# Sampled tokens' high and low parts in one stationary operand: two matmuls instead of three

## The chip, the cores and the metric

The kernel runs on one core of one Trainium2 chip. The metric is the device time of one execution in microseconds. Before the change it was 3355.91 us (median of 3 runs, 3352.63 to 3362.21).

## The reference

One step of a one-layer decoder. There are 2048 prompt tokens and 64 sampled tokens (8 sequences of 8), with a model width of 1024. Both kinds of tokens go through the same weights:

```python
z  = x @ w_in                                  # q, k, v, gates of two kinds of heads
fox_h = softmax(q k^T * scale + decay) @ v     # sampled tokens: over 8192 cached positions, paged
m_h   = mLSTM(q, k, v, gates)                  # chunked matrix memory
x1  = layer_norm(ALPHA * x  + concat(fox_h, norm(m_h) * og) @ w_o)
hid = square(relu(x1 @ w1))                    # width 4096
y   = layer_norm(ALPHA * x1 + hid @ w2)
```

Outputs are `y` for prompt and sampled tokens, the new keys, values and gates, and the memory's states.

## The kernel before

**Precision by three matmuls.** Every operand of a large product is split into a high part in a shorter float format (`split_hi`, an ACT copy, L149) and a low part, the difference (`split_lo`, a DVE subtraction, L152). A product is then made of three matmuls into the same PSUM buffer (`mm3`, L157 to L159): high by high, high by low, low by high. Each matmul has a weight load of its own (PEld in the profile) for the stationary operand, which has one column for each row of the result.

**Tiles.** Prompt tokens make 16 tiles of 128 rows (t = 0 to 15). The 64 sampled tokens are tile 16. Where tokens are the stationary operand, tile 16 uses 64 of the 128 columns.

**Stages.** Block A (`block_a`, four blocks of prompt tokens; the first, `BLKS[0]`, starts with tile 16) makes the input products. Eight passes through `natural` have tokens as the stationary operand and 256 or 272 weight columns moving: two for the memory's values, two for the output gate, two for keys, two for values. For each tile the results go through a PSUM buffer `pm` (four in rotation) to `sink`, which evicts them with ACT (`stage`) or DVE. Between these passes lie eight convolution passes and four query passes with weights as the stationary operand. Phase B is the prompt's attention, phase O its output projection. Phase C is the MLP in four blocks of tiles (`CB`; only the last, 12 to 15, contains tile 16). For each of 16 chunks `fc` of the hidden width, `hidden` (L1382 on) makes 2 x 128 hidden columns, transposed, with the split parts in `hh` and `hl`; `output` (L1398 on) multiplies the chunk before by `w2` for every tile in two halves of 512 columns into a buffer `py` (three in rotation) and adds it to the tile's row `y` (L1422). The last two chunks are put out together, tile by tile, with the layer norm behind each tile; tile 16, the last, has a layer norm of its own in two halves (`last_norm`), whose halves leave from SP's and ACT's queues.

**The sampled tokens' output projection** (`sampled`, L1343 on) stands in the third block of phase C, ahead of its chunk 14, when the sampled attention is done. It uses 8 pieces of `w_o` through the raw buffers `wr` (four) and the split buffers `wh` and `wl`, 4 x 8 products of 256 columns, and a layer norm.

**The sampled attention** (`sample_attention`) is a stream of steps that is put between the matmuls of all other stages at a given pace. Its cached keys come by indirect DMA from POOL's queue (L1597) into a ring `kT`, are transposed by DVE (L1603) and multiplied on PE (L1626); values come the same way (L1714, L1738). A small tile `ri` for the decay uses the ring's memory first.

**Order.** A scheduler orders the instructions of each engine when the kernel is built; buffers that rotate decide who waits for whom.

Of the kernel before, what the change touches and what calls it, by code (L numbers as in the profile page):

```python
# [10 lines left out]
F32 = mybir.dt.float32  # L11
# [3 lines left out]
OP = mybir.AluOpType  # L15
# [37 lines left out]
def body(ctx, tc, I, O, stages):  # L53
# [102 lines left out]
    def mm3(ps, wh, wl, xh, xl, first, stop):  # L156
        T.matmul(ps, wh, xh, start=first, stop=False)  # L157
        T.matmul(ps, wh, xl, start=False, stop=False)  # L158
        last["PE"] = T.matmul(ps, wl, xh, start=False, stop=stop)  # L159

    def layer_norm(x, np_, g, b, wk, tg, eng=None):
        w = wk.tile([128, 64], F32, name="ln", bufs=2)
        st, mv, rs = w[:, 0:12].rearrange("p (i s) -> p i s", i=2), w[:, 16:18], w[:, 24:27]
        for i in range(2):
            V.bn_stats(st[:np_, i], x[:, i * 512:(i + 1) * 512])
        V.bn_aggr(mv[:np_], st[:np_])
        V.tensor_scalar(rs[:np_, 0:1], mv[:np_, 1:2], EPS, None, op0=OP.add)
# [3 lines left out]
        V.tensor_tensor(x, x, g[:np_], op=OP.mult)  # L171
        (eng or G).tensor_tensor(x, x, b[:np_], op=OP.add)
# [33 lines left out]
    pz = es_z.enter_context(tc.tile_pool(name="pz", bufs=1, reuse_waits="tile"))  # L206
    es_a = ExitStack()
    pa = es_a.enter_context(tc.tile_pool(name="pa", bufs=1, reuse_waits="tile"))
    ppa = es_a.enter_context(tc.tile_pool(name="ppa", bufs=1, space=PSUM, reuse_waits="tile"))


# [253 lines left out]
    def block_a(bi):  # L465
# [3 lines left out]
        def natural(sink, *cols, hook=None, after=None):  # L469
            wh, wl = W0.pop() if W0 else wload(cols)  # L470
            for i, t in enumerate(blk):
                if hook:
                    hook(i)
                m = tok_n(t)
                ps = ppa.tile([128, 512], F32, name="pm", tag="pm", bufs=4)[:m, :wh[0].shape[1]]
                (xh, xl), s = xcol(bi, t)
                for k in range(8):
                    mm3(ps, xh[:, k, s], xl[:, k, s], wh[k], wl[k], k == 0, k == 7)
# [5 lines left out]
        def stage(ps, m, n):  # L484
            st = pa.tile([128, 256], F32, name="st", bufs=4)[:m, :n]
            A.copy(st, ps)
            return st

        def turn_next(n):
# [5 lines left out]
        for i in range(2):  # L495
            def sink(t, m, ps, i=i):
                r = tok_r(t)
                SY.dma_start(dv[r:r + m, i * 256:(i + 1) * 256], stage(ps[:, :256], m, 256))
                if i == 1:
                    V.tensor_copy((gats if t == 16 else gat[:, t])[:, 0:16], ps[:, 256:272])  # L500
# [76 lines left out]
        for i in range(2):  # L577
            def sink(t, m, ps, i=i):
                r = tok_r(t)
                cs = slice(i * 256, (i + 1) * 256)  # L580
                st = pa.tile([128, 256], F32, name="st", bufs=4)[:m]
                V.tensor_tensor(st, ps, bog[:m, cs], op=OP.add)
# [28 lines left out]
        for i in range(2):  # L611
            def sink(t, m, ps, i=i):
                d = k_out(t)[:, i * 256:(i + 1) * 256]
                if t == 16:
                    if i == 0:
                        sqk.append(ps_.tile([64, 512], F32, name="sqk", tag="vt", bufs=2))
                    st = sqk[0][:, i * 256:(i + 1) * 256]
                    A.copy(st, ps)
# [302 lines left out]

    gen = None
    if "S" in stages:
        gen = sample_attention(tc, I, O, ps_, pps, cst, ident, sqk, dnl, dR, dmix, dqb, vx, kx, pa)
    x_load(16, 0)
    W0 = [wload([(C_V, 256)])]
    x_turn(0, 16)
# [404 lines left out]
    def phase_c():  # L1332
# [10 lines left out]
        def sampled():  # L1343

            mx = pc.tile([128, 8, 64], F32, name="mxs", tag="hq", bufs=1)
            SY.dma_start(mx, dmv[:, :, S:])
            mh = ph.tile([128, 8, 64], F32R, name="mhs", tag="hh", bufs=4)
            ml = ph.tile([128, 8, 64], F32R, name="mls", tag="hl", bufs=4)
            split_hi(mh, mx)
            split_lo(ml, mx, mh)  # L1350
            y = row()
            SY.dma_start(y[:64], x_of(16))
            for c in range(4):
                ps = ppc.tile([128, 512], F32, name="py", bufs=3)[:64, :256]
# [5 lines left out]
                V.scalar_tensor_tensor(y[:64, s], y[:64, s], ALPHA, ps, op0=OP.mult, op1=OP.add)  # L1360
            layer_norm(y[:64], 64, *vecs(1), pc, "1")
            SY.dma_start(dx1[S:], y[:64])

# [7 lines left out]
        for ci, blk in enumerate(CB):  # L1371
# [7 lines left out]
            def hidden(fc):  # L1379
                w1p = C.pop("w1", None) or w1_pieces(fc)  # L1380
                H[fc] = []
                for f in range(2):  # L1382
                    hh = ph.tile([128, 576], F32R, name="hh", bufs=4)
                    hl = ph.tile([128, 576], F32R, name="hl", bufs=4)
                    H[fc].append((hh, hl))
                    for (a, b) in pieces:
                        ps = ppc.tile([128, 512], F32, name="ph", tag="ph", bufs=3)[:, :b - a]
                        for k in range(8):
# [3 lines left out]
                        A.activation(hq, ps, AF.Relu)  # L1392
                        A.activation(hq, hq, AF.Square)
                        split_hi(hh[:, a:b], hq)
                        split_lo(hl[:, a:b], hq, hh[:, a:b])
                        tick((b - a) * 0.01)

            def output(fcs):  # L1398
                w2p = [piece(w2[fc * 256 + k * 128:fc * 256 + k * 128 + 128].rearrange("(k p) c -> p k c", p=128)) for fc in fcs for k in range(2)]
                h = [x for fc in fcs for x in H.pop(fc)]  # L1400
                if 15 in fcs:
                    gb = vecs(2)
                for t in blk:
                    n = tok_n(t)
                    s = slice(off[t], off[t] + n)
                    if 0 in fcs:
                        ys[t] = row()
                        with tc.issue_after(last["ACT"].ins):
                            A.dma_start(ys[t][:n], dx1[tok_r(t):tok_r(t) + n])
                    for hf in range(2):  # L1410
                        cs = slice(hf * 512, (hf + 1) * 512)
                        ps = ppc.tile([128, 512], F32, name="py", bufs=3)[:n]
                        for k in range(len(h)):
                            wh, wl = (x[:, 0, cs] for x in w2p[k])
                            mm3(ps, h[k][0][:, s], h[k][1][:, s], wh, wl, k == 0, k == len(h) - 1)
                        y = ys[t][:n, cs]
                        if 15 in fcs and t == 16 and hf == 1:
                            last_norm(ys[t][:n], n, *gb, pc, ps, O["y_sample"].rearrange("b t d -> (b t) d"))
# [5 lines left out]
                    if 15 in fcs and t < 16:  # L1424
                        layer_norm(ys[t], n, *gb, pc, "2")
                        SY.dma_start(O["y_prompt"][0, t * 128:(t + 1) * 128], ys[t])

            for fc in range(16):
                if fc == 14:
# [27 lines left out]
    es_s.close()  # L1457


def sample_attention(tc, I, O, ps_, pps, cst, ident, sqk, dnl, dR, dmix, dqb, vx, kx, pa):  # L1460

    nc = tc.nc
    V, A, G, T, SY = nc.vector, nc.scalar, nc.gpsimd, nc.tensor, nc.sync
# [393 lines left out]
```

## Time and profile before

| what | value |
|---|---|
| time, median of 3 runs | 3355.91 us |
| lowest, highest | 3352.63, 3362.21 us |
| profiled execution: span (the page has no other time of it) | 3381.2 us |
| PE busy, matmuls | 3266.7 us, 21564 |
| PE weight loads busy | 2623.4 us |
| DVE busy | 2145.9 us |
| ACT busy | 1413.8 us |
| POOL busy | 869.5 us |
| mean granted clock of PE | 0.988 |

The span is that of one execution with the profiler on. Matmuls overlap, so a matmul's listed duration is longer than the distance to the next one. "L157" is line 157 of the kernel before. In rows of a timeline the columns are start, duration, engine, line, operation, result<-inputs, shapes and count; in brackets stands how long the engine had nothing to do before, and what released it. In grouped rows the numbers are the total busy time, the mean in ns, and the idle time before with its releasers. A row "128*64 128x512" of a matmul has a stationary operand of 64 columns and 512 moving columns.

### The profile page before, as it was taken

What the parts mean: (1) busy time and instruction counts of PE and PEld (TensorE: products, weight loads), DVE (VectorE), ACT (ScalarE), POOL (GpSimd) and SP (SyncE); (2) the same over time, 40 slices, a digit from 0 to 9 for tenths busy, and PEclk for the clock granted to TensorE, in tenths of its full rate; (3) what the DMA queues carried; (4) which work ended last, traced back from release to release, by engine and by line L of the source; (5) the groups of instructions that cost most, each with busy time, mean ns of one, the idle gap of its engine ahead of it and who ended that gap; (6) DMA issues with size and microseconds to landing.
All of it is one profiled execution on the core that took longest, in us unless ns stands there. A gap on an engine that the chain in (4) does not pass through costs nothing. (4 is left out here: it accounts for less than half of the span.)

```text
span 3381.2 us, 57759 instructions
## 1 busy us (share of the span) xinstructions
PE 3266.7 (97%) x21564; PEld 2623.4 (78%) x21564; DVE 2145.9 (63%) x5180; ACT 1413.8 (42%) x2989; POOL 869.5 (26%) x928
## 2 busy tenths in 40 slices
PE   9999999999999999999999999999999999999998
PEld 8998897787866667677777776777777777888886
DVE  5857567556478878655666667666676545644545
ACT  4444245334378888422332333232332323433332
POOL 0112122422332222365423324323243110100001
PEclk9999999999999999999999999999999999999999
DMA  5665765866652322587776768767678545532221
GB/s 172 165 189 179 221 206 180 292 212 219 227 166 81 90 76 61 209 283 245 286 249 244 247 226 299 254 234 270 209 258 289 198 164 160 168 103 83 87 76 66
DMA packets 427232, 646.25 MB, mean 191 GB/s; under 512 B 83148, under 2 KB 320016, under 8 KB 426056
## 3 DMA queue, kind: packets, MB, share of 16 engines
q1 hardware_dynamic: 350184, 363.22, 35.3%
q0 software_dynamic: 74304, 270.57, 21.8%
q10 hardware_dynamic: 2464, 8.78, 0.7%
q8 instruction: 170, 2.79, 0.3%
q14 instruction: 110, 0.90, 0.1%
HBM read 589.63 MB, written 52.83 MB: 190 GB/s over the span
## 5 line engine op out<-in xcount | busy, mean ns | idle before, releaser
L1422 DVE TENSOR_TENSOR y<-y,py 128x512 f32<-128x512 f32 (+1 forms) x475 | 320.5, 681 | 310.7 <-PE py L159 287.4
L149 ACT ACTIVATE wh<-wr 128x1024 fp32r<-128x1024 f32 x268 | 278.1, 1056 | 500.8 <-PE py L159 215.3
L159 PE MATMUL ph<-x1h,wl 128*128 128x512 f32 (+1 forms) x1280 | 452.9, 355 | 7.7 <-DVE wl L152 7.1
L157 PE MATMUL ph<-x1h,wh 128*128 128x512 f32 (+1 forms) x1280 | 454.9, 355 | 3.6 <-ACT wh L149 2.9
L1597 POOL DMA_INDIRECT kT<-cache_k,idxK x256 | 272.5, 1064 | 718.2 <-PE sQ L1626 657.7
L158 PE MATMUL ph<-x1l,wh 128*128 128x512 f32 (+1 forms) x1280 | 454.4, 355 | 0.0
L1603 DVE STREAM_TRANSPOSE kT<-kT 128x512 f32<-128x512 f32 x512 | 330.3, 685 | 177.1 <-DMA kT<-cache_k,idxK 170.5
L157 PE MATMUL py<-wh,hh 128*128 128x512 f32 (+1 forms) x1088 | 431.7, 399 | 6.8 <-DVE y L1420 4.0
L158 PE MATMUL py<-wl,hh 128*128 128x512 f32 (+1 forms) x1088 | 426.4, 392 | 0.6 <-issue 0.6
L159 PE MATMUL py<-wh,hl 128*128 128x512 f32 (+1 forms) x1088 | 426.3, 393 | 0.3 <-issue 0.3
L152 DVE TENSOR_TENSOR wl<-wr,wh 128x1024 fp32r<-128x1024 f32 x268 | 335.0, 1256 | 81.5 <-ACT wh L149 28.6
L157 PE MATMUL pm<-whi,xhT 128*128 128x256 f32 (+2 forms) x1088 | 319.0, 293 | 4.6 <-ACT whi L149 1.7
L158 PE MATMUL pm<-wlo,xhT 128*128 128x256 f32 (+2 forms) x1088 | 313.8, 289 | 0.8 <-DVE wlo L152 0.8
L159 PE MATMUL pm<-whi,xlT 128*128 128x256 f32 (+3 forms) x1088 | 313.5, 288 | 0.0
L157 PEld LDWEIGHTS ph<-x1h,wh 128*128 128x128 f32 x1280 | 241.8, 189 | 42.9 <-issue 5.2
L159 PEld LDWEIGHTS ph<-x1h,wl 128*128 128x128 f32 x1280 | 241.8, 189 | 43.0 <-DVE wl L152 9.4
L158 PEld LDWEIGHTS ph<-x1l,wh 128*128 128x128 f32 x1280 | 241.9, 189 | 36.9 <-issue 4.1
L157 PEld LDWEIGHTS py<-wh,hh 128*128 128x128 f32 (+1 forms) x1088 | 201.3, 185 | 64.4 <-issue 11.9
L159 PEld LDWEIGHTS py<-wh,hl 128*128 128x128 f32 (+1 forms) x1088 | 200.9, 185 | 52.7 <-issue 5.3
L158 PEld LDWEIGHTS py<-wl,hh 128*128 128x128 f32 (+1 forms) x1088 | 201.4, 185 | 40.6 <-issue 2.3
L157 PEld LDWEIGHTS pm<-whi,xhT 128*128 128x128 f32 (+1 forms) x1088 | 207.9, 191 | 13.7 <-issue 7.8
L1072 ACT ACTIVATE S<-S,mx 128x512 f32<-128x512 f32 (+2 forms) x320 | 207.8, 652 | 17.7 <-DVE mx L1060 16.6
(394 smaller groups left out, 6534.9 us busy)
## 6 DMA issues: line engine op xcount, KB each, us to landing
wr<-w SPq DMA_DIRECT2D x256, 512.0 KB
wra<-w_in SPq DMA_DIRECT2D x112, 512.0 KB
Rb<-dR SPq DMA_DIRECT2D x128, 128.0 KB
wr<-w_o SPq DMA_DIRECT2D x16, 512.0 KB
xr<-dmix SPq DMA_DIRECT2D x16, 512.0 KB
y<-x_prompt SPq DMA_DIRECT2D x16, 512.0 KB
dx<-y SPq DMA_DIRECT2D x16, 512.0 KB
xr<-dx SPq DMA_DIRECT2D x16, 512.0 KB
```

The lines of the kernel that those rows point to most:

```text
L149: last["ACT"] = A.activation(dst, src, AF.Copy, scale=scale)
L152: r = (eng or V).tensor_tensor(dst, src, hi.bitcast(F32), op=OP.subtract)
L157: T.matmul(ps, wh, xh, start=first, stop=False)
L158: T.matmul(ps, wh, xl, start=False, stop=False)
L159: last["PE"] = T.matmul(ps, wl, xh, start=False, stop=stop)
L1072: last["ACT"] = A.activation(sp[:, :w], sp[:, :w], AF.Exp, bias=mx[:, 7:8], accum_out=lp[:, k:k + 1])
L1422: V.tensor_tensor(y, y, ps, op=OP.add)
L1597: G.indirect_dma_start(out=piece(n), out_offset=None, in_=ck, in_offset=IO(ap=idxK[:, b, j // 2, j % 2:j % 2 + 1], axis=0))
L1603: V.transpose(x, x)
```

## The change

For tile 16 the high and the low part stand side by side as 64 + 64 columns of one stationary operand. Two matmuls, with the weights' high part and with their low part, then give the products of the high part in PSUM rows 0 to 63 and those of the low part (low by low with them) in rows 64 to 127. The two halves are added behind.

```diff
+    def mm2(ps, whl, xh, xl, first, stop):
+        T.matmul(ps, whl, xh, start=first, stop=False)
+        last["PE"] = T.matmul(ps, whl, xl, start=False, stop=stop)
...
+    pe = es_e.enter_context(tc.tile_pool(name="pe", bufs=1, reuse_waits="tile"))
+    def ring_a():
+        es_e.close()
+        pr = es_a.enter_context(tc.tile_pool(name="pr", bufs=1, reuse_waits="tile"))
+        return pr.tile([128, 2, 2, 1024], F32, name="kT", bufs=1)
...
+            xT["s"] = pe.tile([128, 8, 128], F32R, name="xsT")
...
+            if t == 16:
+                for c, x in enumerate((xh, xl)):
+                    G.tensor_copy(xT["s"][:, hf * 4:hf * 4 + 4, c * 64:c * 64 + 64], x[:, hf * 4:hf * 4 + 4, s])
...
+                    if t == 16 and xT["s"] is not None:
+                        mm2(ps, xT["s"][:, k], wh[k], wl[k], k == 0, k == 7)
+                    else:
+                        mm3(ps, xh[:, k, s], xl[:, k, s], wh[k], wl[k], k == 0, k == 7)
...
-            A.copy(st, ps)
+            A.copy(st, ps[:m])
+            if m < ps.shape[0]:
+                V.tensor_tensor(st, st, ps[64:128], op=OP.add)
...
         kx["new"] = True
+        xT["s"] = None
...
-        ri = pa.tile([128, 8, 129], F32, name="ri", tag="kT", bufs=1)
+        ri = pe.tile([128, 8, 129], F32, name="ri", bufs=1)
...
-    kx["ring"] = pa.tile([128, 2, 2, 1024], F32, name="kT", tag="kT", bufs=1)
+    kx["ring"] = ring_a()
...
-                        mm3(ps, mh[:, kg * 4 + k], ml[:, kg * 4 + k], wh[:, k], wl[:, k], kg + k == 0, kg + k == 4)
+                        mm2(ps, mhl[:, kg * 4 + k], wh[:, k], wl[:, k], kg + k == 0, kg + k == 4)
...
+                V.tensor_tensor(y[:64, s], y[:64, s], ps[64:128], op=OP.add)
...
-                    hh = ph.tile([128, 576], F32R, name="hh", bufs=4)
-                    hl = ph.tile([128, 576], F32R, name="hl", bufs=4)
-                    H[fc].append((hh, hl))
+                    h2 = ph.tile([128, 1152], F32R, name="h", bufs=4)
+                    hh, hl = h2[:, 0:576], h2[:, 640:1152]
+                    H[fc].append((hh, hl, h2[:, 512:640]))
...
-                        split_lo(hl[:, a:b], hq, hh[:, a:b])
+                        e = min(b, 512)
+                        split_lo(hl[:, a:e], hq[:, :e - a], hh[:, a:e])
+                        if b > 512:
+                            split_lo(h2[:, 576:640], hq[:, e - a:], hh[:, e:b])
...
-                for t in blk:
+                for t in (blk[-1:] + blk[:-1] if 15 in fcs and ci == 3 else blk):
...
+                        if t == 16:
+                            V.memset(ys[t][64:128], 0.0)
...
+                            if t == 16:
+                                mm2(ps, h[k][2], wh, wl, k == 0, k == len(h) - 1)
+                            else:
+                                mm3(ps, h[k][0][:, s], h[k][1][:, s], wh, wl, k == 0, k == len(h) - 1)
...
-                        if 15 in fcs and t == 16 and hf == 1:
+                        if 15 in fcs and t == 15 and hf == 1:
...
+                    if 15 in fcs and t == 16:
+                        lo = landing(64)
+                        A.copy(lo, ys[t][64:128])
+                        V.tensor_tensor(ys[t][:64], ys[t][:64], lo, op=OP.add)
```

In the MLP the low rows are summed in rows 64 to 127 of tile 16's `y` over all chunks, and added once at the end (by way of ACT, to the other partitions). In the last output group tile 16 comes first and tile 15 last, and `last_norm` serves tile 15. The two value passes keep three matmuls, since the joint operand's memory is given to the ring of keys (`ring_a`) after the key passes. The gates' and the output gate's evictions get an addition of the same kind as `stage`.

More of the change, by code (lines that the diff above doesn't have):

```diff
@@ L474, in natural @@
                 m = tok_n(t)
-                ps = ppa.tile([128, 512], F32, name="pm", tag="pm", bufs=4)[:m, :wh[0].shape[1]]
+                ps = ppa.tile([128, 512], F32, name="pm", tag="pm", bufs=4)[:m if xT["s"] is None else 128, :wh[0].shape[1]]
                 (xh, xl), s = xcol(bi, t)
                 for k in range(8):
-                    mm3(ps, xh[:, k, s], xl[:, k, s], wh[k], wl[k], k == 0, k == 7)
+                    if t == 16 and xT["s"] is not None:
+                        mm2(ps, xT["s"][:, k], wh[k], wl[k], k == 0, k == 7)
+                    else:
+                        mm3(ps, xh[:, k, s], xl[:, k, s], wh[k], wl[k], k == 0, k == 7)
                 sink(t, m, ps)
@@ L482, in natural, with stage @@
                 tick(2.6)
-        def stage(ps, m, n):
-            st = pa.tile([128, 256], F32, name="st", bufs=4)[:m, :n]
-            A.copy(st, ps)
+        def stage(ps, m, n, st=None):
+            if st is None:
+                st = pa.tile([128, 256], F32, name="st", bufs=4)[:m, :n]
+            A.copy(st, ps[:m])
+            if m < ps.shape[0]:
+                V.tensor_tensor(st, st, ps[64:128], op=OP.add)
             return st
@@ L499, in sink @@
                 if i == 1:
-                    V.tensor_copy((gats if t == 16 else gat[:, t])[:, 0:16], ps[:, 256:272])
+                    V.tensor_copy((gats if t == 16 else gat[:, t])[:, 0:16], ps[:m, 256:272])
+                    if t == 16:
+                        V.tensor_tensor(gats, gats, ps[64:128, 256:272], op=OP.add)
             natural(sink, (C_V + i * 256, 256), *([(C_FF, 8), (C_I, 8)] if i == 1 else []),
@@ L581, in sink @@
                 st = pa.tile([128, 256], F32, name="st", bufs=4)[:m]
-                V.tensor_tensor(st, ps, bog[:m, cs], op=OP.add)
+                V.tensor_tensor(st, ps[:m], bog[:m, cs], op=OP.add)
+                if m == 64:
+                    V.tensor_tensor(st, st, ps[64:128], op=OP.add)
                 A.activation(st, st, AF.Tanh, scale=0.5)
@@ L616, in sink @@
                         sqk.append(ps_.tile([64, 512], F32, name="sqk", tag="vt", bufs=2))
-                    st = sqk[0][:, i * 256:(i + 1) * 256]
-                    A.copy(st, ps)
+                    st = stage(ps, m, 256, sqk[0][:, i * 256:(i + 1) * 256])
                 else:
@@ L923, in body @@
     if "S" in stages:
-        gen = sample_attention(tc, I, O, ps_, pps, cst, ident, sqk, dnl, dR, dmix, dqb, vx, kx, pa)
+        gen = sample_attention(tc, I, O, ps_, pps, cst, ident, sqk, dnl, dR, dmix, dqb, vx, kx, pe, ring_a)
     x_load(16, 0)
@@ L1346, in sampled @@
             SY.dma_start(mx, dmv[:, :, S:])
[L1347 to L1350, printed above, removed]
+            mhl = ph.tile([128, 8, 128], F32R, name="mhs", tag="h", bufs=4)
+            split_hi(mhl[:, :, 0:64], mx)
+            split_lo(mhl[:, :, 64:128], mx, mhl[:, :, 0:64])
             y = row()
@@ L1353, in sampled @@
             for c in range(4):
-                ps = ppc.tile([128, 512], F32, name="py", bufs=3)[:64, :256]
+                ps = ppc.tile([128, 512], F32, name="py", bufs=3)[:, :256]
                 for kg in range(2):
@@ L1409, in output @@
                             A.dma_start(ys[t][:n], dx1[tok_r(t):tok_r(t) + n])
+                        if t == 16:
+                            V.memset(ys[t][64:128], 0.0)
                     for hf in range(2):
                         cs = slice(hf * 512, (hf + 1) * 512)
-                        ps = ppc.tile([128, 512], F32, name="py", bufs=3)[:n]
+                        ps = ppc.tile([128, 512], F32, name="py", bufs=3)
                         for k in range(len(h)):
                             wh, wl = (x[:, 0, cs] for x in w2p[k])
-                            mm3(ps, h[k][0][:, s], h[k][1][:, s], wh, wl, k == 0, k == len(h) - 1)
-                        y = ys[t][:n, cs]
-                        if 15 in fcs and t == 16 and hf == 1:
-                            last_norm(ys[t][:n], n, *gb, pc, ps, O["y_sample"].rearrange("b t d -> (b t) d"))
+                            if t == 16:
+                                mm2(ps, h[k][2], wh, wl, k == 0, k == len(h) - 1)
+                            else:
+                                mm3(ps, h[k][0][:, s], h[k][1][:, s], wh, wl, k == 0, k == len(h) - 1)
+                        y = ys[t][:, cs]
+                        if 15 in fcs and t == 15 and hf == 1:
+                            last_norm(ys[t], n, *gb, pc, ps, O["y_prompt"][0, t * 128:(t + 1) * 128])
                         elif 0 in fcs:
@@ L1423, in output @@
                         tick(1.28 * len(fcs))
-                    if 15 in fcs and t < 16:
-                        layer_norm(ys[t], n, *gb, pc, "2")
-                        SY.dma_start(O["y_prompt"][0, t * 128:(t + 1) * 128], ys[t])
+                    if 15 in fcs and t == 16:
+                        lo = landing(64)
+                        A.copy(lo, ys[t][64:128])
+                        V.tensor_tensor(ys[t][:64], ys[t][:64], lo, op=OP.add)
+                    if 15 in fcs and (t, ci) != (15, 3):
+                        layer_norm(ys[t][:n], n, *gb, pc, "2")
+                        SY.dma_start(O["y_sample"].rearrange("b t d -> (b t) d") if t == 16 else O["y_prompt"][0, t * 128:(t + 1) * 128], ys[t][:n])
             for fc in range(16):
@@ L1457, in body, with sample_attention @@
     es_s.close()
-def sample_attention(tc, I, O, ps_, pps, cst, ident, sqk, dnl, dR, dmix, dqb, vx, kx, pa):
+def sample_attention(tc, I, O, ps_, pps, cst, ident, sqk, dnl, dR, dmix, dqb, vx, kx, pe, ring_a):
     nc = tc.nc
```

3 lines of the change are left out of this document (2 added, 1 removed).

## The prediction

> **What bounds the kernel now.** I read the page's busy shares first, then a table of stages, then the order of time inside the stages that the change touches.
>
> ```profile
> span 3381.2 us, 57759 instructions
> PE 3266.7 (97%) x21564; PEld 2623.4 (78%) x21564; DVE 2145.9 (63%) x5180; ACT 1413.8 (42%) x2989; POOL 869.5 (26%) x928
> core 0: us, PE busy (x) PEld busy (x) DVE busy (x) ACT busy (x) POOL busy (x), PEclk, DMA share, GB/s
> 60.00:80.00 20.00, 20.00 (x151) 19.39 (x150) 18.84 (x50) 11.27 (x31) 0.00 (x0) 1.00 0.35 84
> 3000.00:3366.00 366.00, 366.00 (x2127) 321.77 (x2126) 188.20 (x265) 121.30 (x210) 9.32 (x7) 1.00 0.25 76
> ```
>
> PE is busy for 97% of the span. The page warns that a busy PE is not PE at its peak, so the stage table matters more. From 3000 to 3366 us, which is the MLP of the last block (the only one with the sampled tile), PE is busy 366.00 of 366.00 us at clock 1.00. DVE has 188.20 us of work there and the DMA share is 0.25. Whatever leaves PE in that stage leaves the time, as long as the matmuls that remain keep their pitch. Early in the kernel it is otherwise: between 60 and 80 us DVE is busy 18.84 of 20 us, so DVE is nearly as tight as PE there.
>
> The timed median is 3355.91 us. The profiled execution shows no time of its own but its span of 3381.2 us, 25.3 us (0.75%) above that median. I make the sum against the span and scale the result by 3355.91/3381.2 = 0.9925.
>
> **MLP output, 64 matmuls fewer.** A matmul's own duration overlaps its neighbours', so its cost is the pitch, the distance of starts. The first pair of rows is three steps apart with a stationary operand of 64 columns, the second three steps apart with 128 columns. Both have 512 moving columns.
>
> ```profile
> 3329.70 0.39 PE L159 MATMUL py<-wh,hl 128*64 128x512 f32 x1
> 3330.38 0.39 PE L159 MATMUL py<-wh,hl 128*64 128x512 f32 x1
> 3342.63 0.39 PE L159 MATMUL py<-wh,hl 128*128 128x512 f32 x1
> 3343.31 0.39 PE L159 MATMUL py<-wh,hl 128*128 128x512 f32 x1
> L158 PEld LDWEIGHTS py<-wl,hh 128*128 128x128 f32 x1024 | 192.8, 188 | 37.3 <-issue 2.3
> L158 PEld LDWEIGHTS py<-wl,hh 128*64 128x64 f32 x64 | 8.6, 134 | 3.3
> ```
>
> Both pitches are 0.68/3 = 0.227 us: the moving columns set it, and the wider load (188 ns against 134 ns) stays beside the matmul before it. The sampled tile has 16 chunks x 2 pieces x 2 halves = 64 products; each loses one of three matmuls. Gain: 64 x 0.227 = 14.5 us, all in the stage where PE never pauses.
>
> **Six input passes.** These rows are 22 steps apart in both pairs, with 256 moving columns: first 64 stationary columns, then 128.
>
> ```profile
> 104.81 0.28 PE L158 MATMUL pm<-wlo,xhT 128*64 128x256 f32 x1
> 107.31 0.28 PE L159 MATMUL pm<-whi,xlT 128*64 128x256 f32 x1
> 15.02 0.28 PE L158 MATMUL pm<-wlo,xhT 128*128 128x256 f32 x1
> 17.66 0.28 PE L159 MATMUL pm<-whi,xlT 128*128 128x256 f32 x1
> ```
>
> That is 0.1136 and 0.120 us. A pass of the sampled tile goes from 24 x 0.1136 = 2.73 us to 16 x 0.120 = 1.92 us: 0.81 us gained. [...]
>
> Not all six gains last. In the first pass the pitch is another (eight steps between the first two rows), and the second pass and the stage behind it wait for something that PE does not set:
>
> ```profile
> 10.34 0.41 PE L157 MATMUL pm<-whi,xhT 128*64 128x256 f32 x1
> 12.05 0.41 PE L159 MATMUL pm<-whi,xlT 128*64 128x256 f32 x1
> 29.55 1.11 ACT L149 ACTIVATE whi<-wra 128x1088 fp32r<-128x1088 f32 x1 [3.72 <-DMA wra<-w_in]
> 30.71 0.46 PE L157 MATMUL pm<-whi,xhT 128*64 128x272 f32 x2 [0.94 <-ACT whi L149]
> 92.27 0.19 PE L456 MATMUL mg<-ident,rows 4*64 4x4 f32 x1 [2.51 <-DVE rows L422]
> L981 POOL COPY dup<-dup 128x256 f32<-128x256 f32 x31 | 12.5, 405 | 62.0 <-DMA dup<-k_prompt 46.9 <-PE po L1094 12.4 <-PE pS L1046 2.6
> ```
>
> The first pass could give 8 x 0.214 = 1.7 us. But the second pass's weights come at 29.55 by DMA and PE already waits 0.94 us for them, so that wait would grow by as much. What the second pass gains (0.8 us) runs into the stage where DVE is full and PE waits 2.51 us for it. I take 0 for these two passes; the other bound is -2.5 us. The four POOL copies that fill the joint operand (405 ns each, by the row of that size, 1.6 us together) lie ahead of the first pass, under the same wait for weights. The four later passes (two gate, two key passes, from 104 us on) I count in full: 4 x 0.81 = 3.2 us. Their extra DVE adds follow the tile that comes first in each pass, with four PSUM buffers in rotation, so nobody waits for them.
>
> **Output projection.** 96 matmuls become 64: 96 x 0.1136 - 64 x 0.120 = 3.2 us, if PE bounded it.
>
> ```profile
> 2863.08 2.70 SPq L1196 DMA_DIRECT2D wr<-w_o  x2
> 2868.88 1.06 ACT L149 ACTIVATE wh<-wr 128x1024 fp32r<-128x1024 f32 x1 [1.21 <-DMA wr<-w_o]
> 2869.14 18.78 SPq L1196 DMA_DIRECT2D wr<-w  x7
> 2874.08 0.28 PE L159 MATMUL py<-wh,mls 128*64 128x256 f32 x1
> 2876.26 0.50 PE L157 MATMUL ph<-x1h,wh 128*128 128x512 f32 x1 [1.91 <-ACT wh L149]
> 2878.00:2880.00 2.00, 2.00 (x6) 1.52 (x6) 1.88 (x4) 0.00 (x0) 0.00 (x0) 0.50 0.66 182
> L1360 DVE SCALAR_TENSOR_TENSOR y<-y,py 64x256 f32<-64x256 f32 x4 | 1.6, 406 | 0.0
> ```
>
> The last w_o piece is split at 2868.88, when its DMA lands, and the next w1 load leaves SP at 2869.14, when that stage's splits free a raw buffer; neither waits for these matmuls. PE's last product starts at 2874.08 and PE then stands 1.91 us until w1 is there. Three microseconds saved ahead of this only lengthen that stand. I take 0, between -3.2 us (buffers that come free sooner bring w1 forward by as much) and +1.6 us (the four added DVE evictions, 406 ns each by the row of the present ones, stand ahead of splits). After this stand the clock falls to 0.50 between 2878 and 2880. [...]
>
> **More DVE work in the last block.** Each second low part is split into 224 and 64 columns.
>
> ```profile
> L152 DVE TENSOR_TENSOR hl<-hq,hh 128x288 fp32r<-128x288 f32 x64 | 29.2, 457 | 65.0 <-ACT hh L149 63.1
> L361 DVE TENSOR_TENSOR gt<-gt,gat 128x64 f32<-128x64 f32 x4 | 0.9, 222 | 0.0
> ```
>
> 224 columns cost between 457 x 224/288 = 355 and 457 ns, the 64 columns 222 ns: at most 32 x 0.22 = 7 us more on DVE over the block, which had 178 us free in 366. It is hidden by matmuls. Without that cover 7 us would come back.
>
> **The end.** The sampled tile moves to the front of the last output group, and tile 15 with 128 rows is the last.
>
> ```profile
> 3366.05 0.40 PE L159 MATMUL py<-wh,hl 128*64 128x512 f32 x1
> 3371.39 0.99 POOL L183 TENSOR_TENSOR ln<-ln,nhalf 64x1 f32<-64x1 f32 x1
> 3372.56 1.40 DVE L188 SCALAR_TENSOR_TENSOR y<-y,ln,b 64x512 f32<-64x512 f32 x2
> 3373.99 0.52 ACTq L189 DMA_DIRECT2D y_sample<-y  x1
> L172 POOL TENSOR_TENSOR y<-y,b 128x1024 f32<-128x1024 f32 x32 | 78.7, 2458 | 54.5 <-DVE y L171 52.5 <-DVE ln L167 1.9
> 2892.00:2896.00 4.00, 4.00 (x19) 3.30 (x19) 3.25 (x5) 3.15 (x6) 0.00 (x0) 1.00 0.95 341
> ```
>
> Now the last matmul starts at 3366.05, the power on POOL at 3371.39, the last issue is at 3373.99 and the span ends 7.2 us later. In the built lists of the changed kernel two POOL additions of 2.46 us stand directly ahead of that power, and tile 13's scaling on DVE waits for tile 14's statistics; following the chain by hand with these durations puts the final scaling 6.9 us behind the last matmul instead of 6.5: I say +0.6 us. Twice the bytes, 256 KB more at the fastest rate of these rows, 341 GB/s, are 0.75 us, of which I leave 0.25 to the time between the two issues: +0.5. At the front of that group the sampled tile's two PSUM buffers and tile 12's are all taken when tile 12's second half needs one, and DVE evicts another first: +0.7, about one eviction. Sum +1.8 us, bounds +0.4 and +3.5.
>
> **Sum.** -14.5 - 3.2 + 0 + 0 + 1.8 = -15.9 us: a span of 3365.3 us, and 15.8 us from the median, 3340.1 us. This kernel's measurement can tell about 0.3%, here 10.1 us.
>
> **Rivals.**
> *All of it arrives* (the early passes, w_o, a cheap end): -14.5 - 3.2 - 2.5 - 3.2 + 0.4 = -23.0, so 3333. For it: the built PE lists hold the same side work at the same places, 144 matmuls shorter. Against: the waits at 30.71, 92.27 and 2876.26.
> *Loads set the pace at 256 columns:* 80 products of 2 x 0.188 instead of 3 x 0.1136 us are +2.8 in place of the gains there; -14.5 + 2.8 + 1.8 = -9.9, so 3346. Against it, the pitch of 0.120 with the same load.
> *Slower, through the gathers of the sampled attention.* The ring of keys now lies where the joint operand lay, so its first gathers wait for the second key pass.
>
> ```profile
> 182.64 1.04 POOL L1597 DMA_INDIRECT kT<-cache_k,idxK  x1
> 186.69 0.28 PE L159 MATMUL pm<-whi,xlT 128*64 128x256 f32 x1
> 195.36 1.08 POOL L674 TENSOR_TENSOR r<-r,nhalf 128x4 f32<-128x4 f32 x1 [5.75 <-DVE r L673]
> L1603 DVE STREAM_TRANSPOSE kT<-kT x40: 656/673/714, 240.9 to 383.5; 128x512 f32<-128x512 f32 x40
> ```
>
> They went out at 182.64, and the operand's last reader would start at 186.69, some 3 us sooner after the change. Behind them on POOL stands a power with 5.75 us of idleness ahead of it, and the first transpose is at 240.9, so a delay of up to 4 us meets covers of 5.75 and over 50 us. If it survived all the same, PE being in order, each of the 64 score steps would wait: from 15.9/64 = 0.25 us a step on the gain is gone; at 0.5 us the loss is 32 - 16 = 16, so 3372.
> That the change does not do what it says is excluded by the built lists.
>
> **How the numbers follow.** Forecast 0.76 (0.06 of it short of 10.1 us), all arrives 0.13, loads 0.05, gathers 0.06 (0.04 slower by over 0.3%, 0.02 about even). Faster 0.70 + 0.13 = 0.83; same 0.06 + 0.05 + 0.02 = 0.13; slower 0.04. The forecast's own ends are -14.5 - 3.2 - 2.5 - 3.2 + 0.4 and, with half of the four passes lost, -14.5 - 1.6 + 1.6 + 3.5 = -11, so 3333 to 3345. The three runs lie 3.3 below and 6.3 above their median, which I allow for: 3331 to 3350, with the loads' case inside.
>
> **What would show it.** PE full again in the last block's stage, and that stage shorter by about 14 us; two matmuls per sampled product at 0.227 and 0.120 us; PE's stand ahead of w1 grown from 1.91 to some 4 to 5 us; the first 100 us no shorter; last matmul to last issue about half a microsecond longer. I am wrong if the wide loads stretch the pitch, if PE waits in the last block, or if waits for gathered keys or values grow.

## The result, and the profile after

| | before | after |
|---|---|---|
| first comparison, median of 8 executions each | 3360.17 us | 3344.75 us |
| ratio, 95% interval | | 0.9966 [0.9952, 0.998] |
| two later comparisons, each on another chip, 12 executions against 35 | 3369.95, 3369.79 us | 3363.52, 3359.62 us |
| ratios | | 0.998 [0.9969, 0.9991], 0.9978 [0.9965, 0.9991] |

The change is faster: the medians differ by 15 us in the first comparison and by 6 to 10 us in the later ones, the ratios stand for 11 us and twice 7 us, and no interval contains 1. The forecast was 3340.1 us and 15.8 us of gain; 3344.75 lies in its range. That the first medians come so near to 15.8 us is partly luck, as the ratios show. The size of the single terms took the experiments.

The kernel before was profiled twice more, since the first trace of it, 3381.2 us, is longer than any timed execution of it (the longest is 3378.74). The pages of one of those later executions (`e9_before_third`) and of the changed kernel begin:

```profile
span 3356.7 us, 57759 instructions
PE 3253.0 (97%) x21564; PEld 2614.8 (78%) x21564; DVE 2143.1 (64%) x5180; ACT 1413.7 (42%) x2989; POOL 866.1 (26%) x928
```

```profile
span 3339.1 us, 57487 instructions
PE 3231.6 (97%) x21420; PEld 2604.3 (78%) x21420; DVE 2156.3 (65%) x5225; ACT 1413.0 (42%) x2990; POOL 869.9 (26%) x932
```

144 matmuls are gone, PE is busy 21 us less and DVE 13 us more. A device time is 1.7 us longer than the span of the same execution (3340.76 and 3339.1 us).

The timeline of the changed kernel gives the pitches of the two-matmul products: a gate pass, the output projection, the MLP output.

```profile
104.18 0.27 PE L164 MATMUL pm<-wlo,xsT 128*128 128x256 f32 x1
105.84 0.28 PE L164 MATMUL pm<-wlo,xsT 128*128 128x256 f32 x1
2837.05 0.28 PE L164 MATMUL py<-wl,mhs 128*128 128x256 f32 x1
2838.01 0.28 PE L164 MATMUL py<-wl,mhs 128*128 128x256 f32 x1
3005.34 0.39 PE L163 MATMUL py<-wh,h 128*128 128x512 f32 x1
3005.80 0.39 PE L163 MATMUL py<-wh,h 128*128 128x512 f32 x1
```

They are 14, 8 and 2 steps apart: 0.119, 0.120 and 0.23 us, as forecast from rows of before (0.120 and 0.227). In the last block PE is still never idle for long (windows of the changed kernel, columns as in the prediction's):

```profile
2990.00:3322.00 332.00, 332.00 (x1941) 299.68 (x1940) 179.35 (x277) 113.93 (x201) 6.91 (x6) 1.00 0.26 79
```

### The profile page after: what moved, and what is told of

It reads as the page before. It is cut to its first block, busy times and chain, and to the rows that moved or that the text cites. A ratio compares the mean times of both kernels' runs of the same rounds, so it can differ in the third digit from the quotient of the medians.

```text
span 3339.1 us, 57487 instructions
## 1 busy us (share of the span) xinstructions
PE 3231.6 (97%) x21420; PEld 2604.3 (78%) x21420; DVE 2156.3 (65%) x5225; ACT 1413.0 (42%) x2990; POOL 869.9 (26%) x932
## 5 line engine op out<-in xcount | busy, mean ns | idle before, releaser
L1458 DVE TENSOR_TENSOR y<-y,py 128x512 f32<-128x512 f32 x475 | 320.0, 680 | 275.6 <-PE py L159 260.5
L1643 DVE STREAM_TRANSPOSE kT<-kT 128x512 f32<-128x512 f32 x512 | 330.6, 685 | 206.2 <-DMA kT<-cache_k,idxK 205.3
L157 PE MATMUL py<-wh,h 128*128 128x512 f32 x1024 | 406.5, 399 | 5.9 <-DVE y L1456 4.5
L158 PE MATMUL py<-wl,h 128*128 128x512 f32 x1024 | 400.9, 392 | 0.0
L159 PE MATMUL py<-wh,h 128*128 128x512 f32 x1024 | 400.9, 392 | 0.0
L157 PE MATMUL pm<-whi,xhT 128*128 128x256 f32 (+2 forms) x1040 | 303.1, 291 | 1.6 <-DVE xlT L152 1.0
L159 PE MATMUL pm<-whi,xlT 128*128 128x256 f32 (+2 forms) x1040 | 298.3, 287 | 0.0
L158 PE MATMUL pm<-wlo,xhT 128*128 128x256 f32 (+2 forms) x1040 | 298.1, 287 | 0.0
L157 PEld LDWEIGHTS py<-wh,h 128*128 128x128 f32 x1024 | 192.3, 188 | 61.1 <-issue 11.5
L159 PEld LDWEIGHTS py<-wh,h 128*128 128x128 f32 x1024 | 192.2, 188 | 45.1 <-issue 4.1
L158 PEld LDWEIGHTS py<-wl,h 128*128 128x128 f32 x1024 | 192.4, 188 | 35.8 <-DVE wl L152 0.4
L1754 POOL DMA_INDIRECT vt<-cache_v,idxV x158 | 163.1, 1032 | 194.5 <-PE sO L1778 138.2
```

Source lines behind the costliest of these rows:

```text
L1643: V.transpose(x, x)
L1754: G.indirect_dma_start(out=vt.rearrange("p f c -> p (f c)"), out_offset=None, in_=cv, in_offset=IO(ap=idxV[:, b, (kt % 4) * 4 + kt // 4, f ...
```

## The experiments

Each kernel is compared with the kernel before on the same chip. "Last block" is the time from the first matmul of its hidden products to the last matmul of the kernel; "first stage" that from the start to the first transposition of sampled queries (`sqk`); "end" that from the start of the last matmul to the end of the span.

**e1_before_again.** No edit: is the first trace of before a fair one to sum against?

> The kernel before, once more, for a second trace. Theory P (the forecast: the change takes PE time out of the last block and out of four passes, and nothing else of size): its last block (first matmul of the sampled tile's block to the last matmul) is about 15 us longer than after's, as in the first trace, while the 13 us that the first trace of before lost against after between 600 and 850 us are chance and shrink by at least half. Rival M (the earlier passes shift the gathers of the sampled attention to a better place): those 13 us are there again.

3362.66 us, span 3361.0. Between the first stage and the prompt's first scores this execution took 713.8 us where the first trace of before took 729.5, and 716.7 in the changed kernel. The difference of 13 us that the first two traces showed there is thus one between executions of the same code, not a gain of the change. The last block took 426.8 us (431.5 in the first trace), 12.2 us more than in the changed kernel's first trace, where about 15 were expected.

**e2_mlp_three.** Three matmuls again in the MLP output:

```diff
-mm2(ps, h[k][2], wh, wl, k == 0, k == len(h) - 1)
+mm3(ps[:64], h[k][2][:, 0:64], h[k][2][:, 64:128], wh, wl, k == 0, k == len(h) - 1)
```

> The changed kernel with three matmuls again in the MLP output of the sampled tile, all else (layout, order of the end, passes, w_o) as after. Theory P: 64 x 0.227 = 14.5 us slower than after, all of it between 2950 us and the last matmul; against before 1 to 2 us faster (3.2 - 1.8), ratio to before about 0.9995. Rival M (the middle of the kernel carries the gain): only some 3 to 5 us slower than after, ratio about 0.998.

3368.45 us against 3367.79, ratio 1.001 [0.9993, 1.0027]: without this part nothing is left of the gain. The forecast's 0.9995 lies in the interval, the rival's 0.998 does not. Last block 428.4 us.

**e3_passes_three.** Three matmuls again in the six passes; no joint operand, no POOL copies, no additions there:

```diff
-xT["s"] = pe.tile([128, 8, 128], F32R, name="xsT")
+xT["s"] = None
```

> The changed kernel with three matmuls again in the six input passes, the joint operand not filled. Theory P: 3 to 4 us slower than after (four passes of 0.81 us and something of the first two), visible before 200 us and constant behind; ratio to before about 0.996 to 0.997. Rival M: over 10 us slower than after, the loss lying between 600 and 850 us, ratio about 0.999.

Ratio 0.9974 [0.9959, 0.9988], no worse than the full change (0.998 and 0.9978). The first stage took 208.0 us (changed kernel 205.8), the last block 415.5. So the loss of 3 to 4 us, "constant behind", did not come: it is there at the end of the first stage, and not in the time.

**e4_wo_three.** Three matmuls again in the output projection:

```diff
-mm2(ps, mhl[:, kg * 4 + k], wh[:, k], wl[:, k], kg + k == 0, kg + k == 4)
+mm3(ps[:64], mhl[:, kg * 4 + k, 0:64], mhl[:, kg * 4 + k, 64:128], wh[:, k], wl[:, k], kg + k == 0, kg + k == 4)
```

> The changed kernel with three matmuls again in the sampled tokens' output projection, the joint operand used by halves. Theory P: PE's 3.2 us there lie under the wait for w1, so from the first matmul of that projection to the first of the chunk behind it takes the same within 1 us (after has 1 us more than before there, by the added DVE evictions), and the whole is within 1 us of after, ratio to before about 0.9955. Rival B (buffers come free sooner, so the gain arrives): 3 us slower than after in that stretch.

Ratio 0.9978 [0.9965, 0.9992]. From the last matmul ahead of the projection to the first one behind it: 13.7 us here, 14.4 in the changed kernel, 14.1 in before. So the projection gains nothing. (Up to 2830 us this kernel runs the same code as the changed one, and yet reached that place some 13 us apart from it.)

**e5_after_again.** The changed kernel on another chip.

> The changed kernel once more, on the chip of the next three. Theory P: ratio to before 0.9955 +- 0.0015; in the trace the stretch from the last block's first hidden matmul to the last matmul 413 to 417 us, last matmul to end 16.6 us, and at the start of the sampled output projection PE waits about 1.8 us for the low part on DVE.

Ratio 0.998 [0.9969, 0.9991], above the expected 0.9955 +- 0.0015; first stage 205.4, last block 415.5, end 16.6 us: the same as in its first trace, in a span that is 27 us longer (3366.3). The wait for the low part is 1.8 us, as expected.

**e6_vectors_apart.** The next layer norm's two vectors no longer pass through the ring `wr` of raw weights:

```diff
-g = bcast(I[f"ln{l}_g"], 0, D, f"g{l}", pcw, tag="wr", bufs=4)
+kw = dict(tag="xr", bufs=2) if l == 1 else dict(tag="wr", bufs=4)
+g = bcast(I[f"ln{l}_g"], 0, D, f"g{l}", pcw, **kw)
```

> The changed kernel with the two ln1 vectors of the sampled rows in the landing buffers instead of two of the four raw weight buffers. Theory W (in the output projection PE's saving is eaten by waits for weights, since two raw buffers are held by the vectors): the stand ahead of the chunk behind (2.3 us in after) falls under 0.5 us, no half clock follows it, and the whole gains 2 to 4 us on after. Rival D (the DMA rate itself sets when w1 comes): the stand stays within 1 us of 2.3, nothing gained.

The stretch around the projection takes 12.6 us (14.1 to 14.4 in the changed kernel's three traces), and the one behind it, up to the last block, 55.8 (57.1 to 59.3). PE's stand ahead of the next chunk is 1.2 us, not under 0.5, but no half clock follows it. Ratio 0.9976 [0.9963, 0.9988], a median 2.1 us below e5's on the same chip, with intervals that overlap.

**e7_low_on_pool.** The same, and the low half of the joint operand of the projection is made by POOL:

```diff
-split_lo(mhl[:, :, 64:128], mx, mhl[:, :, 0:64])
+split_lo(mhl[:, :, 64:128], mx, mhl[:, :, 0:64], G)
```

> As the one with the vectors apart, and the low part of the sampled rows is made by POOL instead of DVE. Theory J (the joint operand makes the first matmul of that projection wait for the low part, which stood behind evictions on DVE; three matmuls started with the high part): the wait of 1.8 us at the first such matmul falls under 0.5 us, 1 to 2 us gained on the kernel without this. Rival: w_o's own split is as late (its wait takes the place), within 0.5 us.

12.3 us and 55.8 us; ratio 0.9968 [0.9956, 0.998]. The first product still waits 1.7 us, now for POOL, so the expected gain of this edit did not come; what is better than in the changed kernel is already there in e6.

**e8_end_on_dve.** The same, and in the last group DVE instead of POOL adds the norm's offset for tiles 13 and 14:

```diff
-layer_norm(ys[t][:n], n, *gb, pc, "2")
+layer_norm(ys[t][:n], n, *gb, pc, "2", V if t in (13, 14) and ci == 3 else None)
```

> As the one before, and the last additions of tiles 13 and 14 at the end are made by DVE instead of POOL, so that the last power on POOL has nothing ahead of it. Theory E (of the end's 16.6 us after the last matmul, 1.5 us are POOL additions ahead of the power and DVE work stretched beside them): 15 us or less from the last matmul to the end. Rival: DVE's added work (2 x 1.2 us) takes the place, no gain or up to 1 us lost.

End 16.3 us instead of 16.6, not the 15 that were expected; ratio 0.9978 [0.9967, 0.9988]. DVE's scaling falls from 2.40 to 1.22 us, but the two additions, 1.2 us each, now stand on DVE among the steps of the last norm.

**e9_before_third and e10_all_three.** Before once more; and the changed kernel with three matmuls everywhere (the edits of e2, e3 and e4 together), so that only layout, ring and order of the change are left.

> The kernel before once more, as the null of this group. Ratio 1.000 to itself; its span is to be set beside those of the three others of the group, stage by stage, with the stretches of the gathers told apart from the rest: those have come out up to 13 us apart between executions of the same code.

> The changed kernel with three matmuls again in the MLP output, in the output projection and in all six passes; only what the change moved besides is kept: the joint operand's layout, the vectors' order in the ring, where the additions at the end stand. What is still open is why the measured gain (8 to 11 us by the ratios) is below the sum of the stages that move the same way in every trace (about 15 us). Theory P (chance only: layout and order cost no more than the 1.5 us at the end): last block back at 427 to 431 us, first pass as before, end 16.6; time of before plus 1 to 2 us, ratio 1.0003 to 1.0006. Rival N (the common part costs something in the middle as well, spread over the gather stages): before plus 5 to 8 us, ratio 1.0015 to 1.0025, and the changed kernel beside it 15 us faster.

Ratios 1.0002 [0.9988, 1.0016] and 0.9999 [0.9985, 1.0013]: what the change moves besides costs nothing that the times can tell (the end of e10 is 16.3 us, 1.1 more than before's). The costly common part falls as a theory; it would have asked for 1.0015 or more.

**e11_after_third and e12_best_again.** On the same chip the changed kernel, and e7's version again.

> The changed kernel a third time, beside its three-matmul twin. Theory P: 14 to 16 us under the twin and 13 to 15 us under the kernel before, ratio 0.9955 to 0.9962. Rival N: 14 to 16 us under the twin, 8 to 10 us under the kernel before, ratio 0.997 to 0.9977.

> The changed kernel with the next normalization's vectors in a ring of their own and the low part of the MLP's second half split off on POOL, once more beside the changed kernel. Theory W (the stand ahead of the MLP after the output projection came from vectors in front of the weights): that stage 1.5 to 2 us shorter and the stretch behind it 3 us shorter, 3 to 4 us under the changed kernel in all, ratio to before 0.001 lower than the changed kernel's. Rival: the two differ by less than 1 us.

The text of e12 speaks of the MLP's second half; its code is that of e7, where POOL makes the low part for the projection. 3359.62 us, ratio 0.9978; and 3357.52 us, ratio 0.9968 [0.9957, 0.9979]. Against the three-matmul twin (3367.99) the changed kernel gains 8.4 us, between nothing and the 14 to 16 that both theories expected of that pair. e7's version lies below the changed kernel on both chips, by 4.6 and 2.1 us of medians, where 3 to 4 were expected; the intervals overlap, the stages (68.1 and 68.3 us against 73.4 and 71.4 from the last matmul ahead of the projection to the last block) do not.

The twins e10 and e11 show best where the matmuls' time went. The timeline of e10 at the ends of the stages, with a gather of cached keys between (POOL starts it, DVE transposes what it brings, PE waits for a DVE product behind that transposition):

```profile
208.53 0.62 PE L1575 MATMUL sT<-ident,sqk 64*32 64x64 f32 x8
324.49 1.45 POOL L1624 DMA_INDIRECT kT<-cache_k,idxK  x1 [22.25 <-DVE nq L900]
331.88 1.30 DVE L1630 STREAM_TRANSPOSE kT<-kT 128x512 f32<-128x512 f32 x2 [3.41 <-DMA kT<-cache_k,idxK]
335.17 1.12 PE L924 MATMUL mm<-vx,kws 64*128 64x512 f32 x2 [0.35 <-DVE vx L920]
2922.43 0.29 PE L157 MATMUL ph<-x1h,wh 128*128 128x288 f32 x1
3349.58 0.39 PE L159 MATMUL py<-wh,h 128*128 128x512 f32 x1
```

The same places in e11, the changed kernel:

```profile
205.52 0.62 PE L1588 MATMUL sT<-ident,sqk 64*32 64x64 f32 x8
321.48 1.14 POOL L1637 DMA_INDIRECT kT<-cache_k,idxK  x1 [23.16 <-PE sQ L1666]
330.43 1.30 DVE L1643 STREAM_TRANSPOSE kT<-kT 128x512 f32<-128x512 f32 x2 [4.14 <-DMA kT<-cache_k,idxK]
333.72 1.12 PE L931 MATMUL mm<-vx,kws 64*128 64x512 f32 x2 [1.91 <-DVE vx L927]
2919.93 0.29 PE L157 MATMUL ph<-x1h,wh 128*128 128x288 f32 x1
3334.87 0.39 PE L159 MATMUL py<-wh,h 128*128 128x512 f32 x1
```

The lead of 3.0 us at the end of the first stage is still there when the gather is started (324.49 and 321.48), and half of it is gone when the keys are there (331.88 and 330.43): DVE waits longer for them, and PE, which waits 0.35 us behind DVE in e10, waits 1.91 us here. The last block lasts 427.15 us in e10 and 414.94 in e11.

## Why the prediction was right, step by step

**MLP output (forecast -14.5 us).** It holds: -12.2 us between the twins, and 415.5 us on average in the five traces with the full MLP change and the changed end (e3, e4, e5, e11, the first of after: 414.6 to 416.8) against 428.1 in the five with three matmuls (first of before, e1, e2, e9, e10: 426.7 to 431.5), -12.6. The pitch and the count are right: if the distances from the start of each of tile 16's matmuls to the next start are added up, 192 of them take 43.9 us in e10 and 128 take 29.6 in e11, 14.3 us less. The forecast let all of this arrive, but some 2 us of it come back in the same block: by the same adding up the hidden products take 1.8 us more in e11 (206.8 against 205.1) and the other tiles' products 0.4. Some 1 us of that is new waiting, for split weights and hidden rows (waits of PE in e11's last block, in us in total, times, longest):

```profile
PE ph L159 <- DVE wl L152: 1.4, 2, 0.8
PE ph L157 <- ACT hq L1420: 0.8, 1, 0.8
```

In e10 the same list has 1.3 us in all. The +0.7 us for a PSUM buffer at the front of the last group is in no run alone; e10, which has the new order with three matmuls, has a last block 0.4 us longer than e1 and e9 (427.15 against 426.8). The added DVE splits are in e10 too, so they cost little, as forecast.

**Six passes (forecast 0 for the first two, -3.2 for the four later ones).** The step that failed is that the four later passes count "in full". The matmuls do leave: the first stage is 3.2 us shorter on average where the passes have two (204.8 to 206.2 us in nine traces) than where they have three (208.0 to 209.4 in five). Some 1 us of it is there by 91 us, where the forecast had none: the `mg` matmul that waits for DVE starts at 91.81 us in e9 and at 91.08 in e11, and at 91.9 and 91.0 on average over the five and the nine traces. But the lead goes on into the sampled attention, where PE ends up waiting for a gather. Windows of e11 around it:

```profile
320.00:324.00 4.00, 4.00 (x39) 3.00 (x32) 3.74 (x17) 1.32 (x3) 2.21 (x2) 1.00 1.02 381
324.00:328.00 4.00, 4.00 (x27) 3.11 (x27) 0.64 (x4) 0.71 (x2) 2.01 (x3) 1.00 0.96 284
328.00:332.00 4.00, 3.81 (x32) 3.60 (x31) 1.57 (x4) 1.06 (x1) 0.00 (x0) 1.00 0.92 243
332.00:336.00 4.00, 2.28 (x13) 1.77 (x14) 3.49 (x10) 0.77 (x2) 0.00 (x0) 1.00 1.02 359
```

The DMA engines are full (0.92 to 1.02) while the keys are under way, and a gather started 3 us sooner is not there 3 us sooner: 8.95 us pass from its first issue to the first transposition in e11, 7.39 in e10. Over all traces it is 8.8 us on average with two-matmul passes (7.2 to 10.1, nine traces) and 7.6 with three (7.2 to 8.6, five), and the `mm` matmul behind starts 1.8 us sooner, not 3.2. Why the gather takes longer is open: in e10 the DMA engines are just as full (1.03, 0.98 and 1.05 in the slices from 324 to 336 us). In the first trace of the changed kernel a longer stand of PE, 2.81 us, was followed by a lower clock. The same place there, by timeline and by windows:

```profile
331.59 1.30 DVE L1643 STREAM_TRANSPOSE kT<-kT 128x512 f32<-128x512 f32 x2 [5.87 <-DMA kT<-cache_k,idxK]
334.88 2.07 PE L931 MATMUL mm<-vx,kws 64*128 64x512 f32 x2 [2.81 <-DVE vx L927]
```

```profile
328.00:332.00 4.00, 4.00 (x34) 3.87 (x33) 0.41 (x1) 1.06 (x1) 0.00 (x0) 1.00 0.94 240
332.00:336.00 4.00, 1.20 (x3) 0.61 (x3) 4.00 (x11) 0.00 (x0) 0.00 (x0) 0.82 0.88 330
336.00:340.00 4.00, 4.00 (x17) 3.46 (x16) 3.06 (x7) 1.47 (x2) 0.00 (x0) 0.50 0.31 120
```

Here the whole lead is gone (334.88 against 335.17 in e10), and the stand is followed by a granted clock of 0.50, at which matmuls of 256 columns start 0.213 us apart (16 steps from 337.49 us) where they had started 0.120 apart at 1.00 (25 steps from 328.79). Over 320 to 360 us the granted clock is below 1 in eight of nine traces with two-matmul passes (mean 0.92) and in two of five with three (mean 0.97); over 40 us that is 1.7 us more lost, an estimate from these means, as much as was left of the lead. Not every fall there follows a stand (the last section has one that does not), so how far the passes are the reason is not shown. That the passes bring nothing in the end fits e3 (0.9974 without them, 0.9978 and 0.998 with them); the ratios' intervals alone would also allow 3 us either way.

**Output projection (forecast 0).** The number is 1 us off, the reason half right. The prediction expected PE's stand ahead of `w1` to grow from 1.91 to 4 to 5 us. The first trace of the changed kernel has this instead (waits of PE from 2815 to 2860 us):

```profile
PE ph L157 <- ACT wh L149: 2.3, 1, 2.3
PE py L163 <- DVE mhs L152: 1.8, 1, 1.8
PE py L164 <- DVE wl L152: 0.9, 1, 0.9
PE py L163 <- ACT wh L149: 0.7, 1, 0.7
```

The same list of e10, with the joint operand's layout but three matmuls:

```profile
PE ph L157 <- ACT wh L149: 1.5, 1, 1.5
PE py L159 <- DVE mhs L152: 0.9, 1, 0.9
```

The stand ahead of `w1` is 2.3 us (2.8 in e11), 1.5 in e10; it is 2.3 to 3.3 us in the five traces with two matmuls here and the vectors in their old place (first of after, e2, e3, e5, e11), and 0.9 to 1.9 in the five with three (first of before, e1, e4, e9, e10). The first product now needs the low part at once, since both parts are one operand, and waits 1.8 us for DVE; the rest goes into waits for split weights. From the last matmul ahead of the projection to the last block the five with two take 72.8 us on average, the five with three 71.8. The weak step is the clock: the prediction saw it at 0.50 behind this stand and its sum has no term for more of it. Half clock follows in all five with two, 5.5 us of it on average, and in two of the five with three, 1.4 us on average; by estimate, half of the difference, some 2 us more are lost. Windows of the changed kernel behind the stand, and of the same place in e10, which has no half clock there:

```profile
2846.80:2853.60 6.80, 4.71 (x11) 3.75 (x12) 4.54 (x8) 2.16 (x3) 0.45 (x1) 0.50 0.48 159
```

```profile
2860.00:2875.00 15.00, 13.45 (x73) 11.16 (x72) 7.56 (x12) 5.26 (x5) 0.94 (x2) 1.00 0.47 157
```

What held this stretch besides, the prediction did not see: e6 shows that two vectors of the next layer norm stood in the ring of raw weights ahead of the next loads. With them apart the projection and the stretch behind it take 3 to 5 us less (68.1 to 68.4 us in e6, e7 and e12, 71.4 to 73.4 in the three traces of the changed kernel), without half clock. The waits of e12:

```profile
PE py L163 <- POOL mhs L152: 1.7, 1, 1.7
PE ph L157 <- ACT wh L149: 0.9, 1, 0.9
PE py L163 <- ACT wh L149: 0.2, 1, 0.2
```

**The end (forecast +0.6 for the chain, +0.5 for the bytes).** Measured in all: +1.5 us (15.16 us in all three traces of before, 16.62 in all three of the changed kernel), near the forecast 1.1, but by other terms. Timeline of e9 (before), then of the changed kernel:

```profile
3349.51 0.52 ACTq L189 DMA_DIRECT2D y_sample<-y  x1
```

```profile
3322.43 0.39 PE L159 MATMUL py<-wh,h 128*128 128x512 f32 x1
3323.87 2.35 POOL L177 TENSOR_TENSOR y<-y,b 128x1024 f32<-128x1024 f32 x1 [2.05 <-DVE y L176]
3324.90 2.40 DVE L176 TENSOR_TENSOR y<-y,g 128x1024 f32<-128x1024 f32 x1
3329.68 0.99 POOL L188 TENSOR_TENSOR ln<-ln,nhalf 128x1 f32<-128x1 f32 x1
3330.85 1.40 DVE L193 SCALAR_TENSOR_TENSOR y<-y,ln,b 128x512 f32<-128x512 f32 x2
3332.28 0.36 ACTq L194 DMA_DIRECT2D y_prompt<-y  x1
```

The final scaling starts 8.42 us behind the last matmul, not the 6.9 worked out by hand: `y<-y,g` on DVE took 2.40 us beside POOL's addition, 1.22 in e8 where POOL had none there. The last issue lies 9.85 us behind the last matmul (7.94 in e9, whose last matmul starts at 3341.57), 1.9 us later, where about half a microsecond was to show. From there to the end of the span it is 6.8 us now and was 7.2: the double bytes cost nothing.

**The rivals.** *Loads set the pace* is out by the pitches. *All of it arrives* is out by e3's ratio and by the projection's stretch in e4. *Slower, through the gathers* is out as a loss, but its place was nearly the right one: a gather took back part of the passes' gain, though a later one than it looked at, and one that started sooner, so not because it waited for the ring. With that one of the prediction's own signs of being wrong did show: the waits for gathered keys grew (in the twins DVE's from 3.41 to 4.14 us, PE's behind it from 0.35 to 1.91).

**The sum.** Between the twins' traces the spans differ by 14.3 us, the medians of 12 executions by 8.4, with an interval of about 6 us either way. Added up from the traces: 12.6 us from the MLP, next to nothing from the passes (3.2, of which the gather takes 1.4 and half clock 1.7), 1.0 back around the projection and 1.5 back at the end make some 10 us. That lies in the intervals of all three comparisons, whose ratios stand for 11, 7 and 7 us. Some 3.7 us of half clock, by the estimates above, are already in this sum. The timed executions have a lower clock too: a mean of 0.9893 in e11 against 0.9904 in e10 and 0.9899 in the 35 executions of before beside them, and 0.9890 against 0.9900 on e5's chip; 0.0006 to 0.0011 of 3365 us are 2 to 4 us, an estimate from these clocks. (In the twins' profiled executions it was 0.990 in both.) That the timed executions lose it at these two places is not shown, since they leave no trace, and the variants do not agree on it: e3 with three-matmul passes has 0.9892, e4 with the three-matmul projection 0.9900, and e6, e7, e8 and e12, whose traces have no half clock behind the projection, 0.9885 to 0.9894. So the forecast of 15.8 us was too large by some 3 us for the passes, 2 us for what comes back in the last block and 1 us for the projection.

## What to carry to other kernels

Matmuls that leave a stage in which PE hardly waits are worth nearly their pitch (14.3 us of pitch brought 12 to 13 here). A lead that was carried into a stage where PE waits for gathers was spent there (3.0 us at its start in the twins, 1.5 us behind the gather), so ask of each saving what the next thing to arrive is, up to the next stage that PE alone sets. Two operands that are merged into one become ready together: the first use waits for the later of them (1.8 us here). Profile the kernel before more than once ahead of summing against it, since one stretch here differed by 16 us between executions of the same code (713.8 and 729.5 us).

## What the runs showed of the hardware

- The granted clock fell to 0.50 after a stand of PE of 2.81 us (rows above), and in e11 stayed at 1.00 after one of 1.91 us at the same place. In the first trace of before it was 0.50 after a stand of 1.91 us too, the one ahead of `w1`, so the length of the stand alone did not settle it. The stretch at half clock was 3.41 us long in e7 (319.42 to 322.83 us) and 6.8 us behind the projection in the first trace of the changed kernel (2846.80 to 2853.60). In e7 the clock fell at 319.42 us although PE was busy by the profile for all of the 3.42 us before, and why is open (windows of e7):

```profile
316.00:319.42 3.42, 3.42 (x35) 2.83 (x36) 3.42 (x8) 1.77 (x6) 0.00 (x0) 1.00 0.23 68
319.42:322.83 3.41, 3.41 (x27) 1.36 (x26) 2.36 (x6) 1.32 (x3) 0.00 (x0) 0.50 0.97 367
```

- A DVE product of two tiles of 128x1024 took 2.40 us beside a POOL addition of 2.35 us (first trace of the changed kernel) and 1.22 us without (e8). The product began 1.03 us behind the addition's start (3324.90 and 3323.87) and ended 1.08 us behind its end (3327.30 and 3326.22); why it takes longer there is not shown.
